# Layer 0's MLP: down products by features with the weights stationary, and 1/mean of squares as a row at the end

## The chip, the cores and the metric

The kernel runs on one core of one Trainium2 chip. The engines of the core are TensorE (PE in the profile, with its weight loads as PEld), VectorE (DVE), ScalarE (ACT), GpSimd (POOL) and SyncE (SP, which here only starts transfers). The metric is the device time of one execution in microseconds; the kernel before took a median of 1022.83 us in three runs (1022.65 to 1023.12).

## What is computed

A two-layer encoder over 512 tokens of 1024 features, in fp32. Layer 0 mixes tokens by stick-breaking attention, layer 1 by a gated linear recurrence (RG-LRU); each layer ends with a squared-ReLU MLP of 4096 hidden features. What the change touches is the MLP of layer 0 and the first step of layer 1:

```python
def rms_norm(x, g):
    y = x * rsqrt(mean(x * x, axis=-1) + EPS)
    return y * g

def squared_relu_mlp(h, w1, w2):
    u = relu(h @ w1)
    return (u * u) @ w2

for layer in range(2):
    h = rms_norm(x, norm_mix[layer])
    x = x + (attention(h) if layer == 0 else rglru_block(h))   # rglru_block begins with h @ w_in
    h = rms_norm(x, norm_mlp[layer])
    x = x + squared_relu_mlp(h, mlp_w1[layer], mlp_w2[layer])
return rms_norm(x, norm_final)
```

The factor of the norm is one number per token. Since ReLU and the square are applied to each element, `(u * u) @ w2` may be computed from x without the factor, and the product multiplied by 1/mean of squares, token by token, at its end. That is how both kernels do it.

## The kernel before

**Precision and layout.** Every matrix product is made of fp32 numbers split in two halves of a shorter type (`wh`, `wl` of the weights; a high and a low half of the activations), and takes three matmuls: high × high, low × high, high × low. Activations are held by features: `x[c]` is a tile of 128 features by 512 tokens, eight tiles in all, and tokens fall into a lower and an upper half of 256.

**The MLP.** It runs in four quarters of the hidden features. Each quarter does its up products (x to hidden) and its down products (hidden to output) by a scheme with seven products of half-size blocks, P1 to P7, in place of eight. The seven down products of a quarter are made in two pieces each (`g` is 0 or 1), in the order P1 0, P5 0, P1 1, P2 0, P5 1, P6 0, P6 1, P3 0, P3 1, P7 0, P7 1, P2 1, P4 0, P4 1: 14 pieces a quarter, 56 in layer 0. Each product ends in a PSUM bank pair named X, V or W, and is collected into one of four accumulators: P1 and P2 into `c[0]`, P6 and P3 into `c[1]`, P4 into `c[2]`, P5 and P7 into `c[3]`. P1, P6, P7 and P4 build on the same bank pair X one after the other, so the next of them can start only when the one before is collected.

**Down pieces before.** `part` (L1175, matmul at L1190) has the activations stationary and 512 columns of weights moving: 12 matmuls a piece, with a result of tokens by features. `collect` (L1154) adds the PSUM bank, times the factor of each token (a column of `rr`, one number per partition), to `c[out]` on VectorE; the first collect of an accumulator is a scaled copy on ScalarE (L1163). Layer 1's MLP uses the same functions (`mixed`) and keeps them in the change.

**The end of the MLP before.** The last product P4 of the last quarter is made in two halves of tokens by `times` (L1140, matmul at L1149). `feature(c)` (L1518) then brings one feature tile back: four TensorE transposes (L1522) of 128 by 128 into a PSUM bank, `add_x` (L764) adds them to x[c] on VectorE, and `halves` (L132) makes the high half `xgh` on ScalarE (L135) and the low half `xgl` on VectorE (L136) for the next product. Tiles 4 to 7 are done between the two halves of P4; tiles 0 to 3 inside the next stage, as entries of the table that `beside` (L246) takes. Squares for the next norm are summed by `squares.chunk` (L153), partly on GpSimd (L162).

**What follows.** `beside` makes the first two slabs of layer 1's input projection (`w_in`, matmuls at L234 to L236, slab casts at L227 and L229), feature tiles in the order 4 to 7, 0 to 3; then a third slab into another bank, with the norm's sum over features (L1655) inside it.

**What sets the order.** TensorE's order is as written. On VectorE and ScalarE of the MLP, `Ordered` (L784) puts each instruction behind the one before it, so they run in the order of the code as well; all its operations show the one line L793. Weights arrive by transfers on SyncE's queue; the sums of weight blocks that P7 and P4 need arrive partly by accumulating transfers that GpSimd issues (L1131). x waits in DRAM (`away`, written by `between` at L1540) during the MLP and is loaded again at L1547 in the last quarter. An operand made of weights lies at a column offset of 0, `UP_AT` = 16 or `OPEN_AT` = 36 in a slightly larger tile.

## Time and profile before

| | |
|---|---|
| timed, median of 3 runs | 1022.83 us |
| the profiled execution | 1023.47 us |
| span of its trace | 1021.7 us |
| granted TensorE clock | 0.998 of full |
| HBM traffic | 140.56 MB read, 6.29 MB written |

The span is what the trace covers from the first to the last instruction; the profiled execution's own time lies 1.8 us above it. The profile lists the busy time of each engine, a chain of work (followed back from the last instruction, at each step to what released it), groups of instructions by line, and a timeline of each engine. In a timeline row stand the start, the duration, the engine, the line, the operation and its tiles; a bracket gives the idle time ahead of the row and what ended it. Where a row says x2, the duration covers two instructions. Durations include a part in which the engine can already start its next instruction, so rows follow each other a little closer than they last.

### The profile page before, as it was taken

The page shows a single profiled execution, that of the slowest core. Times are in us where ns is not written, and L with a number is a line of the kernel's source. Part 1 is how long each engine was busy: PE and PEld are TensorE (multiplying, and loading weights), DVE is VectorE, ACT ScalarE, POOL GpSimd, SP SyncE. Part 2 cuts the span into 40 slices and gives each one's busy share as a digit, 9 for nine tenths or more (in the row PEclk, how much of TensorE's full clock was granted, in tenths as well). Part 3 has the DMA queues.
Part 4 walks back from the last instruction along what each step waited for, and adds up shares of the span by engine and source line. Part 5 has one row for each costly group of instructions (what it writes and reads, how often), then busy time and mean ns, then how long its engine had stood idle before and what let it go on. Part 6 is the DMA issues. An engine that isn't in the chain of part 4 may idle for free.

```text
span 1021.7 us, 16053 instructions
## 1 busy us (share of the span) xinstructions
PE 1013.0 (99%) x5930; PEld 890.1 (87%) x5930; DVE 868.3 (85%) x1165; ACT 701.5 (69%) x1081; POOL 175.5 (17%) x239
## 2 busy tenths in 40 slices
PE   9999999999999999999999999999999999999997
PEld 8888888888888988988988888888988988988986
DVE  7988787848789799799799888899898898898897
ACT  7777676835767764764775799966873763873866
POOL 0454344420000011011011221100010010010012
PEclk9999999999999999999999999999999999999999
DMA  7745454537536666676783476446767667667653
GB/s 237 222 122 145 115 152 102 152 111 262 160 81 198 166 156 195 166 158 194 166 230 90 118 192 173 116 170 200 214 112 206 165 143 202 173 142 201 168 106 111
DMA packets 58719, 165.73 MB, mean 162 GB/s; under 512 B 6928, under 2 KB 12304, under 8 KB 58640
## 3 DMA queue, kind: packets, MB, share of 16 engines
q1 hardware_dynamic: 47264, 124.41, 37.5%
q0 software_dynamic: 10944, 39.85, 23.4%
q8 instruction: 47, 0.77, 0.3%
q10 hardware_dynamic: 432, 0.44, 0.1%
q14 instruction: 32, 0.26, 0.1%
HBM read 140.56 MB, written 6.29 MB: 144 GB/s over the span
## 4 chain that ended last, share of the span: by engine, by line
PE 93%; ACT 3%; DVE 2%; DMA 1%; issue 1%; POOL 0%; ACTq 0%; DVEq 0%
PE ps_t L1190 16%; PE ps_acc L1055 9%; PE ps_acc L1190 9%; PE ps_z L1055 8%; PE ps_acc L234 5%; PE ps_acc L236 5%; PE ps_acc L235 5%; PE ps_o L1055 5%; PE ps_z L1190 4%; PE ps_t L234 2%; PE ps_t L236 2%; PE ps_t L235 2%; PE ps_o L234 2%; PE ps_o L236 2%; PE ps_o L235 2%; PE ps_t L628 2%
## 5 line engine op out<-in xcount | busy, mean ns | idle before, releaser
L793 ACT CAST wh<-b 128x1024 fp32r<-128x1024 f32 x174 | 180.3, 1051 | 121.6 <-DVE b L793 76.7
L793 DVE TENSOR_TENSOR wl<-b,wh 128x1024 fp32r<-128x1024 f32 x174 | 210.4, 1220 | 38.7 <-ACT wh L793 37.5
L1131 POOL DMA_DIRECT2D b<-in_w_dn x40 | 35.0, 875 | 295.3 <-DVE b L793 198.6
L234 PE MATMUL ps_acc<-xgh,wh 128*128 128x512 f32 x192 | 78.4, 408 | 0.0
L793 ACT ACTIVATE u<-u 128x512 f32<-128x512 f32 x103 | 64.9, 632 | 15.3 <-DVE u L793 13.5
L236 PE MATMUL ps_acc<-xgl,wh 128*128 128x512 f32 x192 | 75.2, 392 | 0.0
L235 PE MATMUL ps_acc<-xgh,wl 128*128 128x512 f32 x192 | 75.1, 391 | 0.0
L1131 POOL DMA_DIRECT2D b<-in_w_up x26 | 22.7, 872 | 291.7 <-DVE b L793 100.7
L606 DVE TENSOR_TENSOR_SCAN scan<-keep,later 128x128 f32<-128x128 f32 (+1 forms) x64 | 58.7, 918 | 15.4 <-POOL w L600 7.6
L793 DVE TENSOR_TENSOR b<-b,b 128x1024 f32<-128x1024 f32 x50 | 61.2, 1224 | 1.3
L610 POOL TENSOR_TENSOR w<-w,scan 128x128 f32<-128x128 f32 (+1 forms) x64 | 53.0, 830 | 53.4 <-DVE scan L606 48.8
L793 DVE TENSOR_TENSOR u<-u 128x512 f32<-128x512 f32 (+1 forms) x89 | 55.0, 618 | 4.4 <-ACT u L793 2.5
L229 DVE TENSOR_TENSOR wl<-raw,wh 128x512 fp32r<-128x512 f32 (+2 forms) x64 | 54.3, 877 | 4.1 <-ACT wh L227 4.0
L793 ACT CAST wh<-raw 128x1024 fp32r<-128x1024 f32 x49 | 51.2, 1048 | 6.8 <-PE ps_acc L1190 2.9
L227 ACT CAST wh<-raw 128x512 fp32r<-128x512 f32 (+2 forms) x64 | 44.4, 732 | 14.8 <-PE ps_acc L236 7.3
L1055 PE MATMUL ps_z<-xgh,wh 128*128 128x256 f32 x216 | 50.6, 277 | 0.2
L793 DVE TENSOR_TENSOR wl<-raw,wh 128x1024 fp32r<-128x1024 f32 x39 | 48.0, 1230 | 0.8 <-ACT wh L793 0.8
L1190 PE MATMUL ps_t<-wh,bh 128*128 128x512 f32 x120 | 47.0, 392 | 0.0
L1190 PE MATMUL ps_t<-wh,bl 128*128 128x512 f32 x120 | 46.8, 390 | 0.0
L600 POOL TENSOR_SCALAR_AFFINE_SELECT w<-w 128x128 f32<-128x128 f32 x64 | 32.9, 513 | 69.9 <-ACT w L595 69.7
L1055 PE MATMUL ps_acc<-low,wh 128*128 128x256 f32 x192 | 44.7, 276 | 0.0
L793 DVE TENSOR_TENSOR sl<-u,sh 128x512 fp32r<-128x512 f32 (+2 forms) x53 | 37.9, 716 | 7.7 <-ACT sh L793 7.7
(419 smaller groups left out, 3215.9 us busy)
## 6 DMA issues: line engine op xcount, KB each, us to landing
b<-in_w_dn SPq DMA_DIRECT2D x48, 512.0 KB, 4.3
b<-in_w_dn POOLq DMA_DIRECT2D x40, 512.0 KB, 5.6
b<-in_w_up SPq DMA_DIRECT2D x39, 512.0 KB, 4.6
b<-in_w_up POOLq DMA_DIRECT2D x26, 512.0 KB, 5.5
raw<-in_w_dn SPq DMA_DIRECT2D x16, 512.0 KB, 4.6
raw<-in_w_in SPq DMA_DIRECT2D x16, 512.0 KB, 3.7
raw<-in_w_up SPq DMA_DIRECT2D x13, 512.0 KB, 4.0
raw<-in_w_qk SPq DMA_DIRECT2D x12, 512.0 KB, 3.8
```

The costliest lines, as they stand in the source:

```text
L227: e[0].copy(wh[:, k, :], raw[:, k, :])
L229: e[1].tensor_tensor(wl[:, k, :], raw[:, k, :], f(wh[:, k, :]), ALU.subtract)
L234: PE.matmul(ps, wh, ah, start=start, stop=False)
L235: PE.matmul(ps, wl, ah, start=False, stop=False)
L236: PE.matmul(ps, wh, al, start=False, stop=stop)
L600: G.affine_select(t, t, pattern=[[-1, P]], compare_op=ALU.is_gt, fill=0.0, base=0, channel_multiplier=1,)
L606: V.tensor_tensor_scan(sc[:, S - n : S][:, ::-1], keep[:, :n][:, ::-1], later[:, S - n :][:, ::-1], 1.0, ALU.mult, ALU.max,)
L610: G.tensor_tensor(wt, wt, sc[:, S - n + 1 : S + 1], ALU.mult)
L793: ins = getattr(self.e, name)(*args, **kwargs)
L1055: PE.matmul(ps[:, i * HS : (i + 1) * HS], m, y, start=new and i == k == low == 0 and y is h, stop=(low, i, k) == steps[-1], skip_group_che ...
L1131: G.dma_start(out=unit[b].rearrange("p j n -> p (j n)"), in_=unit["src"](to), accum_op=ALU.add)
L1190: PE.matmul(sums[to][i], a[:, j, block, i * P : (i + 1) * P], y[:, j, :], start=new and g == j == n == 0 and a is h, stop=g == j == 1 and ...
```

## The change

In layer 0 alone (`not self.mixed`), the down products are turned round. `across` takes 128 by 128 blocks of weights as the stationary operand and 256 tokens of activations as the moving one: 24 matmuls of 256 columns a piece instead of 12 of 512. The result is by features, as x is, so no transposes remain (`feature` goes). The factor of a token then no longer belongs to a partition but to a column: `keep_factors` stores the factors in DRAM, `back` loads them as a row repeated on all 128 partitions (`rr`), and the accumulators, now summed without factors by plain additions and subtractions, are multiplied by that row once, in the last quarter, and added to x in blocks. `done(name)` does this after P6 (c[2], on GpSimd, with its four additions to x), after P3 (c[1], likewise), after P7 (c[3], product on VectorE) and after P2 (c[0], product on GpSimd; the additions of c[3] on VectorE). P4's own result is multiplied in PSUM and added by VectorE in `end`. GpSimd's MLP work, transfers included, becomes `Ordered` too.

```diff
--- before.py
+++ after.py
@@ -832,7 +832,8 @@
         def __init__(self, ctx, layer, squares=None):
             self.layer, self.sq, self.first = layer, squares or Squares(), None
             self.mixed = squares is not None
-            self.V, self.A = Ordered(V), Ordered(A)
+            self.V, self.A, self.G = Ordered(V), Ordered(A), Ordered(G)
+            self.G.turn(not self.mixed)
             self.mp = ctx.enter_context(tc.tile_pool(name=f"mlp{layer}", bufs=2))
             self.u = {}
             if self.mixed:
...
@@ -1136,6 +1137,23 @@
 
         FAR = "P7", "P4"
 
+
+        def across(self, name, g, i, w, ps, new=False, ends=True, rounds=None):
+
+            block = self.PRODUCTS[name][0]
+            (wh, wl), (h, l) = w, self.a[g]
+            rounds = rounds or [((h, wh), (l, wh)), ((h, wl),)]
+            for n, pairs in enumerate(rounds):
+                for jj in range(2):
+                    for a, y in pairs:
+                        for k in range(2):
+                            f0 = (2 * i + k) * P
+                            PE.matmul(
+                                ps[:, k * HS : (k + 1) * HS], y[:, jj, f0 : f0 + P], a[:, jj, block, :],
+                                start=new and n == jj == k == 0 and a is h,
+                                stop=ends and (n, jj, k) == (len(rounds) - 1, 1, 1),
+                                skip_group_check=name not in ("P1", "P5", "P2"),
+                            )
 
         def times(self, name, g, i, w, ps, new, cols=slice(0, S)):
 
@@ -1154,6 +1172,14 @@
         def collect(self, name, i, ps, cols=slice(0, S)):
             out, less = self.PRODUCTS[name][4:]
             y = self.c[out][:, i, cols]
+            if not self.mixed:
+                if (out, i) in self.begun:
+                    op = ALU.subtract if less else ALU.add
+                    self.gained = self.V.tensor_tensor(y, y, ps, op)
+                else:
+                    self.begun.add((out, i))
+                    A.activation(y, ps, AF.Identity, scale=1.0 - 2.0 * less)
+                return
             t = NB * less + out // 2 * 2 + i
             scale = self.rr[:, t : t + 1]
             if (out, i) in self.begun:
@@ -1183,6 +1209,14 @@
             rounds = ((h, wh), (l, wh)), ((h, wl),)
             if (name, g) == ("P1", 1):
                 rounds = ((h, wh),), ((h, wl),), ((l, wh),)
+            if not self.mixed:
+                for n in range(len(rounds)):
+                    for i in range(2):
+                        self.across(
+                            name, g, i, w, sums[to][i], new and g == n == 0,
+                            g == 1 and n == len(rounds) - 1, rounds[n : n + 1],
+                        )
+                return
             for n, pairs in enumerate(rounds):
                 for i in range(2):
                     for j in range(2):
@@ -1246,7 +1280,7 @@
                     return
                 name = steps[i][3]
                 kind, q4, p, name = steps[i]
-                at = 0
+                at = 0 if self.mixed else self.OPEN_AT if i == 0 else UP_AT
                 if kind == "up":
                     at = self.OPEN_AT if i == 0 or (p, name) == (0, "P1") else UP_AT
                 ws[i] = made[i] = self.operand(self.source(unit(i), name), at)
@@ -1324,6 +1358,8 @@
                     if p:
                         for n in range(2):
                             self.collect(name, n, bank[n])
+                        if not self.mixed and q4 == NQ - 1:
+                            end.done(name)
                     if not ahead:
                         prepare_or_hold(i)
                     if begin:
@@ -1457,9 +1493,13 @@
                 if new:
                     banks[to] = self.bank()
                 self.up(name, ws.pop(i), banks[to], new)
+            rest = [ws[len(steps) - 2 + g] for g in range(2)], sums["down", NQ - 1, 0]["X"]
+            if not self.mixed:
+                end(*rest)
             for e in (self.V, self.A):
                 e.turn(False)
-            end([ws[len(steps) - 2 + g] for g in range(2)], sums["down", NQ - 1, 0]["X"])
+            if self.mixed:
+                end(*rest)
 
         def mixed_quarters(self, residues, gains, end):
             self.gains = gains
@@ -1497,6 +1537,7 @@
                         self.sq.chunk(n, x[n], e=V)
                 if c == C - 2:
                     self.rr = self.sq.inv_squares(self.bank())
+                    between.factors(self.rr)
                 between(c)
 
                 k = c - 4
@@ -1515,48 +1556,106 @@
         squares = Squares()
         last = {}
 
-        def feature(c, tag):
-
...
+        factors = dram.tile([1, S], F32, tag="factors", name="factors")
+        lo, hi = slice(0, HS), slice(HS, S)
+        rr = []
+
+        def keep_factors(cols):
+            nc.sync.dma_start(
+                out=factors.rearrange("o (t p) -> p (o t)", p=P), in_=cols[:, :NB]
+            )
+
+        def back():
+            for c in (*range(4), *range(4, C)):
+                x[c] = home_tile(*HOMES[c], "x")
+                nc.sync.dma_start(out=x[c], in_=away[:, c, :])
+                if c == 0:
+                    rr.append(mlp.mp.tile([P, S], F32, tag="low", name="rr", bufs=1))
+                    nc.sync.dma_start(out=rr[0], in_=factors.broadcast_to([P, S]))
+
+        def times_factors(e, y, ts):
+            n = y.shape[1] // HS
+            y = y.rearrange("p (k n) -> p k n", k=n)
+            e.tensor_tensor(y, y, rr[0][:, ts].unsqueeze(1).broadcast_to([P, n, HS]), ALU.mult)
+
+        def add_block(e, out, ks=range(4)):
+            h, ts = out % 2, (lo, hi)[out // 2]
+            for k in ks:
+                xc = x[4 * h + k][:, ts]
+                e.tensor_tensor(xc, xc, mlp.c[out][:, k // 2, k % 2 * HS : (k % 2 + 1) * HS], ALU.add)
+
+        def block(out):
+            times_factors(mlp.G, mlp.c[out].rearrange("p i n -> p (i n)"), (lo, hi)[out // 2])
+            add_block(mlp.G, out)
+
+        def done(name):
+            if name == "P6":
+                block(2)
+            elif name == "P3":
+                block(1)
+            elif name == "P7":
+                times_factors(mlp.V, mlp.c[3].rearrange("p i n -> p (i n)"), hi)
+            elif name == "P2":
+                times_factors(mlp.G, mlp.c[0].rearrange("p i n -> p (i n)"), lo)
+                add_block(mlp.V, 3)
+
+        def high(*cs):
+            for c in cs:
+                mlp.A.activation(
+                    xgh[:, c, :], x[c], AF.Identity, scale=col("mix1")[:, c : c + 1]
                 )
-            add_x(c, pt)
-            last["low"] = halves("mix1", c, x[c])
+
+        def low(*cs):
+            for c in cs:
+                last["low"] = mlp.V.scalar_tensor_tensor(
+                    xgl[:, c, :], x[c], col("mix1")[:, c : c + 1], f(xgh[:, c, :]),
+                    ALU.mult, ALU.subtract,
+                )
+
+        def square(*cs):
+            for c in cs:
+                squares.chunk(c, x[c], e=G, a=mlp.A)
 
         def end(ws, xs):
             for i in range(2):
                 for g in range(2):
-                    mlp.times("P4", g, i, ws[g], xs[i], False)
-                mlp.collect("P4", i, xs[i])
...
+                    mlp.across("P4", g, i, ws[g], xs[i], ends=g == 1)
+
+            def add_last(i):
+                for k in range(2):
+                    xc = x[2 * i + k][:, hi]
+                    mlp.V.tensor_tensor(xc, xc, xs[i][:, k * HS : (k + 1) * HS], ALU.add)
+
+            high(4, 5, 6, 7)
+            low(4, 5)
+            add_block(mlp.V, 0, range(2))
+            low(6, 7)
+            square(4, 5)
+            times_factors(mlp.V, xs[0], hi)
+            add_last(0)
+            high(0)
+            square(6)
+            high(1)
+            times_factors(mlp.V, xs[1], hi)
+            add_block(mlp.V, 0, range(2, 4))
+            add_last(1)
+            low(0, 1)
+            square(7)
+            high(2, 3)
+            low(2, 3)
 
         def between(c):
             nc.sync.dma_start(out=away[:, c, :], in_=x[c])
             if c == C - 1:
                 soft.send(mlp.ready)
 
-        def back():
-            for c in range(C):
-                x[c] = home_tile(*HOMES[c], "x")
-                nc.sync.dma_start(out=x[c], in_=away[:, c, :])
-
-        end.ready = back
+        between.factors = keep_factors
+        end.ready, end.done = back, done
         mlp.quarters(between, end)
 
         begin = [bank("acc") for _ in range(2)]
         beside(
-            [slab(w_in[C + i]) for i in range(2)], xgh, xgl, begin,
-            {
-                1: lambda: [feature(c, "z") for c in range(2)],
-                2: lambda: [feature(c, "o") for c in range(2, 4)],
-            },
-            (*range(4, C), *range(4)),
+            [slab(w_in[C + i]) for i in range(2)], xgh, xgl, begin, {}, (*range(4, C), *range(4)),
         )
         behind[0] = last["low"].ins
         third = slab(w_in[C + 2])
```

Three places show how the instructions now stand. First VectorE at the end of the last quarter, from the collects of P7 on; `x_6399` to `x_6405` are x[4] to x[7], `ps_t` is bank pair X, `ps_z` W. Before:

```order
L793 SCALAR_TENSOR_TENSOR c3_3173<-ps_t_5913,rr_3514,c3_3173 128x512
L793 SCALAR_TENSOR_TENSOR c3_3173<-ps_t_5914,rr_3514,c3_3173 128x512
L229 TENSOR_TENSOR wl_6202<-raw_6199,wh_6201 128x1024
L793 SCALAR_TENSOR_TENSOR c0_3170<-ps_z_5973,rr_3514,c0_3170 128x512
L793 SCALAR_TENSOR_TENSOR c0_3170<-ps_z_5974,rr_3514,c0_3170 128x512
L229 TENSOR_TENSOR wl_6208<-raw_6205,wh_6207 128x1024
L793 SCALAR_TENSOR_TENSOR c2_3172<-ps_t_5913,rr_3514,c2_3172 128x512
L765 TENSOR_TENSOR x_5891<-x_5891,ps_z_6140 128x512
L765 TENSOR_TENSOR x_5893<-x_5893,ps_z_6150 128x512
L765 TENSOR_TENSOR x_5895<-x_5895,ps_o_6161 128x512
L765 TENSOR_TENSOR x_5897<-x_5897,ps_o_6172 128x512
L136 SCALAR_TENSOR_TENSOR xgl_83<-x_5891,colt_70,xgh_82 128x512
```

and now:

```order
L793 TENSOR_TENSOR c3_3173<-c3_3173,ps_t_6421 128x512
L793 TENSOR_TENSOR c3_3173<-c3_3173,ps_t_6422 128x512
L229 TENSOR_TENSOR wl_6886<-raw_6883,wh_6885 128x1024
L793 TENSOR_TENSOR c3_3173<-c3_3173,rr_6391 128x1024
L793 TENSOR_TENSOR c0_3170<-c0_3170,ps_z_6517 128x512
L793 TENSOR_TENSOR c0_3170<-c0_3170,ps_z_6518 128x512
L229 TENSOR_TENSOR wl_6892<-raw_6889,wh_6891 128x1024
L793 TENSOR_TENSOR x_6399<-x_6399,c3_3173 128x256
L793 TENSOR_TENSOR x_6401<-x_6401,c3_3173 128x256
L793 TENSOR_TENSOR x_6403<-x_6403,c3_3173 128x256
L793 TENSOR_TENSOR x_6405<-x_6405,c3_3173 128x256
L793 SCALAR_TENSOR_TENSOR xgl_83<-x_6399,colt_70,xgh_82 128x512
```

The collects lose their factor; the multiplication of c[3] comes in behind the first `wl`, and the additions to x[4] to x[7] are of SBUF operands, 256 wide, and stand ahead of P4's result instead of behind transposes.

Second GpSimd, from the last weight transfers to layer 1. Before:

```order
L1131 DMA b11_5530<-in_w_dn 128x1024
L1131 DMA b11_5534<-in_w_dn 128x1024
L162 TENSOR_TENSOR ssq_6148<-ssq_6148,sq_6158 128x512
L162 TENSOR_TENSOR ssq_6148<-ssq_6148,sq_6169 128x512
L162 TENSOR_TENSOR ssq_6148<-ssq_6148,sq_6180 128x512
L1585 MEMSET gh_6324 128x768
L1585 MEMSET gl_6325 128x768
```

and now:

```order
L793 DMA b11_6040<-in_w_dn 128x1024
L793 TENSOR_TENSOR c2_3172<-c2_3172,rr_6391 128x1024
L793 TENSOR_TENSOR x_6389<-x_6389,c2_3172 128x256
L793 TENSOR_TENSOR x_6393<-x_6393,c2_3172 128x256
L793 TENSOR_TENSOR x_6395<-x_6395,c2_3172 128x256
L793 TENSOR_TENSOR x_6397<-x_6397,c2_3172 128x256
L793 TENSOR_TENSOR c1_3171<-c1_3171,rr_6391 128x1024
L793 TENSOR_TENSOR x_6399<-x_6399,c1_3171 128x256
L793 TENSOR_TENSOR x_6401<-x_6401,c1_3171 128x256
L793 TENSOR_TENSOR x_6403<-x_6403,c1_3171 128x256
L793 TENSOR_TENSOR x_6405<-x_6405,c1_3171 128x256
L793 TENSOR_TENSOR c0_3170<-c0_3170,rr_6391 128x1024
```

Behind the same last transfer three products of 1024 and eight additions of 256 are put in; the sums of squares follow as before.

Third ScalarE, from the casts of the `w_in` slabs to the high halves of x[4] to x[7]. Before:

```order
L227 CAST wh_6201<-raw_6199 128x1024
L227 CAST wh_6207<-raw_6205 128x1024
L135 ACTIVATE xgh_82<-x_5891,colt_70 128x512
L157 ACTIVATE ssq_6148<-x_5891 128x512
L135 ACTIVATE xgh_82<-x_5893,colt_70 128x512
L160 ACTIVATE sq_6158<-x_5893 128x512
L135 ACTIVATE xgh_82<-x_5895,colt_70 128x512
L160 ACTIVATE sq_6169<-x_5895 128x512
L227 CAST wh_6293<-raw_6291 128x1024
L135 ACTIVATE xgh_82<-x_5897,colt_70 128x512
```

and now:

```order
L227 CAST wh_6885<-raw_6883 128x1024
L227 CAST wh_6891<-raw_6889 128x1024
L227 CAST wh_6945<-raw_6943 128x1024
L793 ACTIVATE xgh_82<-x_6399,colt_70 128x512
L793 ACTIVATE xgh_82<-x_6401,colt_70 128x512
L793 ACTIVATE xgh_82<-x_6403,colt_70 128x512
L793 CAST wh_7017<-raw_6982 128x1024
L793 ACTIVATE xgh_82<-x_6405,colt_70 128x512
L793 ACTIVATE ssq_6853<-x_6399 128x512
L793 ACTIVATE sq_6855<-x_6401 128x512
```

The third cast has moved ahead of the high half of x[4], and the squares behind the high halves.

17 lines of the change are left out of this document (4 added, 13 removed).

## The prediction

> **What bounds the kernel now.** First the page: which engine is busy, and which engine the last chain of work runs over.
>
> ```profile
> span 1021.7 us, 16053 instructions
> PE 1013.0 (99%) x5930; PEld 890.1 (87%) x5930; DVE 868.3 (85%) x1165; ACT 701.5 (69%) x1081; POOL 175.5 (17%) x239
> PE 93%; ACT 3%; DVE 2%; DMA 1%; issue 1%; POOL 0%; ACTq 0%; DVEq 0%
> ```
>
> TensorE (PE) is busy 99% of the span and carries 93% of the chain. So there are two ways to change the time: take matmul time away, or make PE wait where it doesn't wait now. The second is open because VectorE (DVE) is busy 85% on average and may be full where the change lies. I therefore read the chain in order of time around the end of layer 0's MLP (start, duration, work).
>
> ```profile
> 539.01 5.57 PE ps_acc L1190 x24
> 544.58 5.44 PE ps_t L1190 x24
> ...
> 552.74 2.72 PE ps_t L1149 x12
> 555.46 0.87 PE ps_z L1522 x8
> 556.34 0.87 PE ps_o L1522 x8
> 557.21 2.75 PE ps_t L1149 x12
> 559.96 0.23 PE ps_acc L234
> ...
> 561.32 0.87 PE ps_z L1522 x8
> ...
> 563.58 0.87 PE ps_o L1522 x8
> ...
> 572.66 0.23 PE ps_t L234
> ```
>
> The reader is to see that PE has no gap: the last down products (L1190), P4 in two halves (L1149), four groups of transposes (L1522), then at 559.96 the first matmul of layer 1's input projection (L234), and at 572.66 the first of its third slab. One row of 5.57 instead of 5.44 is a small wait.
>
> Then VectorE over the same stretch, from its timeline.
>
> ```profile
> 537.97 1.41 DVE L793 SCALAR_TENSOR_TENSOR c<-ps_acc,rr,c 128x512 f32<-128x512 f32 x2
> 539.28 0.68 DVE L793 TENSOR_TENSOR sl<-u,sh 128x512 fp32r<-128x512 f32 x1
> 539.88 1.22 DVE L793 TENSOR_TENSOR wl<-b,wh 128x1024 fp32r<-128x1024 f32 x1
> 541.02 0.68 DVE L793 TENSOR_TENSOR sl<-u,sh 128x512 fp32r<-128x512 f32 x1
> 541.62 1.22 DVE L793 TENSOR_TENSOR wl<-b,wh 128x1024 fp32r<-128x1024 f32 x1
> 542.76 1.41 DVE L793 SCALAR_TENSOR_TENSOR c<-ps_t,rr,c 128x512 f32<-128x512 f32 x2
> 544.08 1.22 DVE L793 TENSOR_TENSOR wl<-b,wh 128x1024 fp32r<-128x1024 f32 x1
> 545.21 1.22 DVE L793 TENSOR_TENSOR wl<-raw,wh 128x1024 fp32r<-128x1024 f32 x1
> 546.35 1.41 DVE L793 SCALAR_TENSOR_TENSOR c<-ps_acc,rr,c 128x512 f32<-128x512 f32 x2
> 547.66 2.35 DVE L793 TENSOR_TENSOR wl<-b,wh 128x1024 fp32r<-128x1024 f32 x2
> 549.93 1.41 DVE L793 SCALAR_TENSOR_TENSOR c<-ps_t,rr,c 128x512 f32<-128x512 f32 x2
> 551.25 1.22 DVE L229 TENSOR_TENSOR wl<-raw,wh 128x1024 fp32r<-128x1024 f32 x1
> 552.38 1.41 DVE L793 SCALAR_TENSOR_TENSOR c<-ps_z,rr,c 128x512 f32<-128x512 f32 x2
> 553.71 1.22 DVE L229 TENSOR_TENSOR wl<-raw,wh 128x1024 fp32r<-128x1024 f32 x1
> ```
>
> No row shows idle time in brackets: VectorE is full for 16 us, one instruction behind the other, and it is the engine to which the change adds work just there. From start to start a 512 row takes 0.60, a 1024 row 1.14, a pair of collects 1.31. GpSimd (POOL), which gets the rest of the new work, is idle there:
>
> ```profile
> 559.35 3.48 POOL L162 TENSOR_TENSOR ssq<-ssq,sq 128x512 f32<-128x512 f32 x2 [21.15 <-ACT sq L160]
> ```
>
> **The matmuls.** Each of the 56 down pieces of layer 0 becomes 24 matmuls of 256 columns, where it was 12 of 512. The old piece costs 5.44 / 2 = 2.72 (the x24 row holds two pieces). The up pieces are 24 matmuls of 256 already, with weights stationary, as the new ones will be:
>
> ```profile
> 432.60 2.72 PE ps_o L1055 x24
> 726.84 2.87 PE ps_z L1055 x24
> ```
>
> So 2.72 for 2.72: I take nothing for this part. The other end is 0.15 for each of 56 pieces, +8.4 us, if all ran like the second row. That is one of the few up pieces whose weights lie 36 columns into their tile; the new pieces use the other offset except the very first, so I stay at the first row.
>
> The Trainium skill (TensorE: Matmul & The Clock Gate, "Wait — 56ns, not 53.3ns?") puts a fixed 2.5 ns on each matmul of a warm array. By that rule 12 more matmuls a piece would cost 30 ns, 1.7 us in all; the rows with 2.72 on both sides don't show it.
>
> **What goes.** The four groups of transposes go: 4 × 0.87 = 3.48 us on the path, 1.74 ahead of 559.96 and 1.74 behind it. The collects become plain additions of one PSUM operand and one SBUF operand; at the 0.60 of a 512 row a pair takes 1.20, where it took 1.31. That shortens the small waits of the kind of 5.57 (three of about 0.1 in the trace), some 0.3 in all, hidden elsewhere by PE's full rows.
>
> **What comes.** The factor row goes through DRAM on the sync queue: one small store early in the MLP and one broadcast load beside the reloads of x (about 512). It has 25 us until its first use, about 538; nothing for it. If it came later than that, GpSimd alone would wait.
>
> On GpSimd: c2 × factors (1024 elements a partition), four additions of 256 into x, c1 × factors, four additions, c0 × factors. On VectorE: c3 × factors and twelve 256-wide additions, two multiplications in PSUM. The trace prices GpSimd's two-operand work at up to 512 elements:
>
> ```profile
> L610 POOL TENSOR_TENSOR w<-w,scan 128x512 f32<-128x512 f32 x16 | 18.3, 1142 | 15.3 <-DVE scan L606 14.8
> L610 POOL TENSOR_TENSOR w<-w,scan 128x384 f32<-128x384 f32 x16 | 15.9, 992 | 18.7 <-DVE scan L606 17.6 <-DMA raw<-in_w_qk 1.0
> L738 POOL TENSOR_TENSOR x<-x,early 128x512 f32<-128x512 f32 x2 | 2.6, 1292 | 9.4 <-DMA x<-in_xT 9.4
> ```
>
> With about 0.19 fixed, this is 1.86 ns an element by the first row ((1142 − 190) / 512; some 1.76 in its undisturbed instances) and 2.15 by the third: a 1024 product 2.0 to 2.4 us, a 256 addition 0.64 to 0.74. From 384 to 512 the w rows grow by only 1.17 ns an element, the low end. The third row has the new work's form (in place, added to x), and I take 2.15.
>
> Alone this would be hidden. It isn't alone: GpSimd and VectorE hold each other up. When GpSimd worked on 512 elements at 92.06, the VectorE instruction that began at 92.41 took 1.58, where its like take 0.68:
>
> ```profile
> 92.06 1.39 POOL L610 TENSOR_TENSOR w<-w,scan 128x512 f32<-128x512 f32 x1 [1.69 <-DVE scan L606]
> L229 DVE TENSOR_TENSOR wl<-raw,wh x4: 668/683/1584, 91.8 to 95.7; 128x512 fp32r<-128x512 f32 x4
> ```
>
> (Columns of the second: minimum, median, maximum in ns.) That is 0.90 longer, nearly all that GpSimd had left (1.04). It goes both ways, but not for VectorE instructions with an operand in PSUM:
>
> ```profile
> 1001.96 1.99 POOL L793 TENSOR_TENSOR c<-c,gb 128x512 f32<-128x512 f32 x1 [5.12 <-ACT junk L1858]
> 1008.50 1.50 POOL L793 TENSOR_TENSOR c<-c,gb 128x512 f32<-128x512 f32 x1 [4.54 <-ACT junk L1858]
> ...
> 1002.72 1.41 DVE L793 SCALAR_TENSOR_TENSOR c<-ps_t,rr,c 128x512 f32<-128x512 f32 x2
> ```
>
> Here the pair from PSUM took its usual 1.41 beside GpSimd (whose 1.99 waited for a wl row first; alone it takes 1.50, which is 2.56 ns an element, the high end). So I read: of two-operand instructions with both operands in SBUF one engine runs at a time; GpSimd holds VectorE off for its duration less about 0.2 (2.2 for a product, 0.55 for an addition). In the stretch above, wl and sl rows are of that kind, collects aren't.
>
> The Trainium skill (GPSIMD Engine Reference, section 8, "Key points") says that the two share their SBUF interfaces and contend on VectorE instructions with two SBUF inputs: the rows just quoted agree. Its section 3.1 gives 2.6 cycles an element at 1.2 GHz for such work, 2.17 ns: the x row agrees, the w rows are below it and the c row above. By 2.17 the sum below would stay as it is.
>
> **The sum.** When does x[4], the first operand of the input projection, have its last addition (c3's)? In the new order VectorE does, from the sl at 539.17 (0.1 earlier by a cheaper collect): 2 sl × 0.60 + 8 wl × 1.14 + 8 collects × 0.60 + c3 × factors 1.14 + one 256 addition 0.4 (half of 0.60, and the 0.1 by which a row outlasts its start-to-start). 1.20 + 9.12 + 4.80 + 1.14 + 0.4 = 16.7, so 555.9 undisturbed. Holds by GpSimd on top: c2's product begins near 537.8, beside the collects of 537.97, and holds the sl for 1.0; three of c2's additions 3 × 0.55 = 1.65 (the fourth falls beside the collects from PSUM); c1's product 2.2; of its additions 0.6, the rest beside collects; c0's product 2.2, right ahead of the addition that x[4] waits for. Together 7.65: 563.5. (By the w rows' 1.76, products hold 1.8 and additions 0.45: 0.6 + 1.35 + 1.8 + 0.5 + 1.8 = 6.05, 1.6 less.) Then the high half of x[4] on ScalarE:
>
> ```profile
> 556.88 0.72 ACT L135 ACTIVATE xgh<-x,colt 128x512 fp32r<-128x512 f32 x1 [3.96 <-DVE x L765]
> 558.56 1.41 DVE L136 SCALAR_TENSOR_TENSOR xgl<-x,colt,xgh 128x512 fp32r<-128x512 f32 x2
> ```
>
> 0.63 of the 0.72 go by until the next can start: the input projection begins at about 564.1, where it began at 559.96: **+4.1**. PE meanwhile, which would be ready 1.74 earlier, waits: some 1.9 ahead of P7 (the bank of X is free only when c1's late collect is done), 1.0 ahead of P4, 3.6 ahead of the projection.
>
> Behind it, PE ran 572.66 − 559.96 = 12.70 to the third slab, 1.74 of it transposes: 10.96 stay. The low half of x[4] comes 0.5 after the first high matmuls want it (0.75 for a row like the xgl one). x[0]'s is the next risk: from xgl of x[4] to xgl of x[0] VectorE has about 7.9 us of rows (the halves, c0's additions, PSUM products and P4's additions, one hold by a square's sum), PE 6.4 us of matmuls: 1.6 of wait. 564.1 + 10.96 + 0.5 + 1.6 = 577.2, against 572.66: **+4.5**; a tenth more for the norm behind the later squares: **+4.6**. From there PE was full before and is full after: the 4.6 stay to the end. The profiled execution took 1023.47 in all (span 1021.7 and 1.8 around it), 0.64 above the median of the runs shown, 1022.83. 1023.47 + 4.6 = 1028.1 for a profiled run, **1027.4** for the median.
>
> **The rivals.**
>
> *GpSimd gets in nobody's way* (the holds are much shorter for these shapes, or VectorE goes first). Then x[4] is ready near 556.6 and the projection waits only for the cast of the third w_in slab, which ScalarE does ahead of the high halves and which waits for P4's first weights: about 558.2, so −1.74 is kept, about 1.1 of wait for x[0] eats the larger part of the second 1.74, and the 0.3 comes on top: −2.3, **1020.5**, faster. For it: the transposes are real matmul time, and PE bounds. Against it: the three holds quoted. 0.12.
>
> *Shorter holds*, from the low end of 1.17 ns an element up to 1.7: at the low end products hold 1.2 and additions 0.3, c2's product none, together 0.9 + 1.2 + 0.3 + 1.2 = 3.6, 4 less than above: +0.6; up to +2.5 at 1.7. **1024**. 0.13.
>
> *Longer holds*, the high end of 2.56 ns (the c row is a product too): products hold 2.6, additions 0.65, together 1.4 + 1.95 + 2.6 + 0.8 + 2.6 = 9.35, 1.7 more than above; and as VectorE falls behind, up to four more additions meet wl rows instead of collects, 2.6 more. +6.3 to +8.9, **1031**. 0.09.
>
> *Dearer narrow matmuls*: +8.4 by the 2.87 row on top of a sum at either price of GpSimd, **1034**. 0.03.
>
> *The change doesn't do what it says*: if the orders kept the transposes' place filled with another wait, it is the sum above; nothing in the order leaves the transposes in. No chance of its own.
>
> **How the numbers follow.** The forecast (holds of 1.76 to 2.4 ns) has 0.63, 1025.8 to 1029.5. What a measurement of this kernel can tell is about 0.2%, 2.05 us: faster is below 1020.8, slower above 1024.9. Of the no-contention case most is faster, 0.12 with a little of its upper half at same; of the short-hold case two thirds lie within: same 0.10; the rest, 0.78, is slower. The range takes the forecast, the short holds and the better part of the long ones, and leaves out the no-contention case and the narrow matmuls: 1023.0 to 1031.0.
>
> **What would show it.** No transposes, and down pieces of 24 still at 2.72; GpSimd products of 2.0 to 2.4 (3.3 where they wait for VectorE); wl rows of 1.7 to 3.4 instead of 1.22 between 538 and 558; PE waits ahead of P7, of P4, and of 3 to 4 us ahead of the projection's first matmul, released by ScalarE's high half; that matmul at 564 and the third slab at 577. The prediction is wrong if wl rows stay at 1.22 beside busy GpSimd, if the projection starts before 560, or if down pieces leave 2.72.

## The result, and the profile after

The changed kernel took a median of 1028.93 us (1028.61 to 1029.88, 4 runs), the kernel before 1022.98 us (1022.65 to 1023.28, 4 runs): a ratio of 1.0061 with a 95% interval of 1.0046 to 1.0075, 5.95 us slower. The profiled execution took 1029.19 us, 5.72 more than that of before. Every time in this document leaves out one slow execution, the first one of the kernel `vector_psum` further down, which took 5827.59 us with TensorE at about a sixth of its speed.

The page of the kernel after, the lines that answer to the first ones of before:

```profile
PE 1012.8 (99%) x6570; PEld 915.3 (89%) x6570; DVE 874.2 (85%) x1170; ACT 700.8 (68%) x1081; POOL 194.7 (19%) x250
PE 91%; DVE 4%; ACT 2%; DMA 1%; issue 1%; POOL 0%; SPq 0%; DVEq 0%; ACTq 0%
```

The busy time says almost nothing: PE 1012.8 against 1013.0, although 3.48 us of transposes are gone. GpSimd was busy 19 us longer, its own waits for VectorE included. The chain tells more: VectorE's share went from 2% to 4%, and ScalarE's and PE's shrank. Where PE waited, from the view of its waits (line, what it waited for, us in total, times, longest), two rows of the MLP's end are new:

```profile
PE ps_acc L234 <- ACT xgh L793: 3.3, 1, 3.3
PE ps_t L1151 <- DVE c L793: 2.2, 2, 1.8
```

The chain in order of time shows where VectorE stands on it:

```profile
539.67 3.08 PE ps_acc L1151 x24
542.78 0.97 DVE wl L793
...
546.58 0.61 DVE c L793
547.32 2.72 PE ps_t L1151 x22
...
562.10 3.48 DVE x L793 x4
565.59 0.67 DVE xgl L793
...
581.39 0.86 PE ps_z L1754 x2
```

and the norm's matmuls in the same view of the kernel before:

```profile
575.38 0.86 PE ps_z L1655 x2
```

They begin at 581.39 instead of 575.38: 6.01 late, as much as the whole loss. Then VectorE and GpSimd over that stretch, from their timelines:

```profile
538.84 1.28 DVE L793 TENSOR_TENSOR c<-c,ps_acc 128x512 f32<-128x512 f32 x2
540.03 2.03 DVE L793 TENSOR_TENSOR sl<-u,sh 128x512 fp32r<-128x512 f32 x1
541.99 1.76 DVE L793 TENSOR_TENSOR wl<-b,wh 128x1024 fp32r<-128x1024 f32 x1
543.67 1.22 DVE L793 TENSOR_TENSOR sl<-u,sh 128x512 fp32r<-128x512 f32 x1
544.82 1.76 DVE L793 TENSOR_TENSOR wl<-b,wh 128x1024 fp32r<-128x1024 f32 x1
...
551.16 4.57 DVE L793 TENSOR_TENSOR wl<-b,wh 128x1024 fp32r<-128x1024 f32 x2
...
558.02 1.75 DVE L793 TENSOR_TENSOR c<-c,rr 128x1024 f32<-128x1024 f32 x1
...
562.02 3.56 DVE L793 TENSOR_TENSOR x<-x,c 128x256 f32<-128x256 f32 x4
```

```profile
538.76 2.75 POOL L793 TENSOR_TENSOR c<-c,rr 128x1024 f32<-128x1024 f32 x1
541.59 5.57 POOL L793 TENSOR_TENSOR x<-x,c 128x256 f32<-128x256 f32 x4
551.32 3.33 POOL L793 TENSOR_TENSOR c<-c,rr 128x1024 f32<-128x1024 f32 x1 [4.16 <-DVE c L793]
554.72 5.64 POOL L793 TENSOR_TENSOR x<-x,c 128x256 f32<-128x256 f32 x4
561.04 3.25 POOL L793 TENSOR_TENSOR c<-c,rr 128x1024 f32<-128x1024 f32 x1 [0.68 <-DVE c L793]
```

Read the two against each other: while GpSimd's first product runs (538.76 to 541.51), VectorE's collects from PSUM keep their 1.28 a pair, and the first instruction with two SBUF operands behind them takes 2.03 instead of 0.68. During the four additions the wl rows take 1.76 instead of 1.22 and the sl row 1.22 instead of 0.68; during the second product two wl rows take 4.57 instead of 2.35; during the third four additions of 256 take 3.56. And GpSimd is slowed by VectorE as well: an addition takes 1.4 on average, about twice the 0.64 to 0.74 that it was priced at alone.

Last, what was not forecast: windows (us, busy time of PE, PEld, DVE, ACT, POOL, then the granted clock, DMA share, GB/s) around the start of the input projection at 565.44:

```profile
562.16:565.43 3.27, 0.01 (x1) 0.00 (x0) 3.27 (x4) 0.77 (x2) 2.14 (x1) 1.00 0.50 160
565.43:570.60 5.17, 5.03 (x14) 3.70 (x15) 5.14 (x11) 4.33 (x7) 1.27 (x1) 0.67 0.01 3
```

and the same columns for two stretches of 3.41 us:

```profile
563.64:567.05 3.41, 1.48 (x5) 0.97 (x6) 3.41 (x7) 2.39 (x4) 0.66 (x1) 1.00 0.34 130
567.05:570.46 3.41, 3.41 (x9) 2.64 (x9) 3.38 (x8) 2.57 (x5) 1.17 (x1) 0.50 0.00 0
```

PE idles for 3.27 us, and over the next 5.17 its clock is 0.67 on average: it goes on at 1.00 until 567.05 and then runs at 0.50 for 3.41 us, so that 1.7 us of matmul time are lost.

### The profile page after: what moved, and what is told of

It reads as the page before. It is cut to its first block, busy times and chain, and to the rows that moved or that the text cites. A ratio compares the mean times of both kernels' runs of the same rounds, so it can differ in the third digit from the quotient of the medians.

```text
span 1027.4 us, 17362 instructions
## 1 busy us (share of the span) xinstructions
PE 1012.8 (99%) x6570; PEld 915.3 (89%) x6570; DVE 874.2 (85%) x1170; ACT 700.8 (68%) x1081; POOL 194.7 (19%) x250
## 4 chain that ended last, share of the span: by engine, by line
PE 91%; DVE 4%; ACT 2%; DMA 1%; issue 1%; POOL 0%; SPq 0%; DVEq 0%; ACTq 0%
PE ps_acc L1056 9%; PE ps_z L1056 8%; PE ps_t L1224 8%; PE ps_t L1151 8%; PE ps_acc L236 5%; PE ps_acc L234 5%; PE ps_acc L235 5%; PE ps_o L1056 5%; PE ps_acc L1224 4%; PE ps_acc L1151 4%; PE ps_t L234 2%; PE ps_t L236 2%; PE ps_t L235 2%; PE ps_z L1224 2%; PE ps_z L1151 2%; PE ps_o L234 2%
## 5 line engine op out<-in xcount | busy, mean ns | idle before, releaser
L793 DVE TENSOR_TENSOR wl<-b,wh 128x1024 fp32r<-128x1024 f32 x174 | 213.9, 1240 | 40.5 <-ACT wh L793 40.3
L234 PEld LDWEIGHTS ps_acc<-xgh,wh 128*128 128x128 f32 x192 | 36.6, 190 | 8.7 <-ACT xgh L793 3.5
L236 PEld LDWEIGHTS ps_acc<-xgl,wh 128*128 128x128 f32 x192 | 36.3, 189 | 8.7 <-DVE xgl L793 0.7
```

The lines of the kernel that those rows point to most:

```text
L234: PE.matmul(ps, wh, ah, start=start, stop=False)
L236: PE.matmul(ps, wh, al, start=False, stop=stop)
L793: ins = getattr(self.e, name)(*args, **kwargs)
```

## The experiments

### GpSimd's blocks left out of the change

```diff
-            if name == "P6":
-                block(2)
-            elif name == "P3":
-                block(1)
+            if name in ("P6", "P3"):
+                pass
...
-                times_factors(mlp.G, mlp.c[0].rearrange("p i n -> p (i n)"), lo)
```

> The changed kernel without the GpSimd blocks: the products of c[0], c[1], c[2] with the factor row and the additions of c[1] and c[2] to x are left out (so x is not the reference's). Theory A (GpSimd holds VectorE off whenever both have two operands in SBUF): the wl rows between 540 and 556 go back to 1.14 to 1.22, x[4] is complete some 7.9 us earlier (the sum of the holds in the trace after), the projection waits only for the third w_in cast and begins near 559 to 560, its clock stays at 1.00; 1021.5 to 1023. Rival B (VectorE's own new rows and the new order on ScalarE make the projection late, GpSimd is beside the point): the projection still begins after 563; 1027 or more. Rival C (the narrow matmuls cost it): 1027 or more, with PE waits gone.

Measured: 1022.50 us (1021.24 to 1025.32, 10 runs), a ratio to before of 0.9998 [0.9988, 1.0007]. The rows of VectorE between 539 and 556 are back at their usual durations (timeline of this run):

```profile
539.35 0.68 DVE L793 TENSOR_TENSOR sl<-u,sh 128x512 fp32r<-128x512 f32 x1
539.95 1.22 DVE L793 TENSOR_TENSOR wl<-b,wh 128x1024 fp32r<-128x1024 f32 x1
...
547.49 2.35 DVE L793 TENSOR_TENSOR wl<-b,wh 128x1024 fp32r<-128x1024 f32 x2
...
552.12 1.22 DVE L793 TENSOR_TENSOR c<-c,rr 128x1024 f32<-128x1024 f32 x1
...
555.59 1.42 DVE L793 TENSOR_TENSOR x<-x,c 128x256 f32<-128x256 f32 x4
```

The waits ahead of P7, P4 and the projection are gone; the one left is of 1.4 us, for the low half of x[0]. So GpSimd's blocks carry the loss, 6.4 us, as A says; B and C fall. But the kernel isn't faster than before either, though work is missing: in this order of things the change can't win even without those blocks.

### GpSimd's blocks added to the kernel before

```diff
+        def same(y):
+            n = y.shape[1] // P
+            y = y.rearrange("p (k n) -> p k n", k=n)
+            mlp.G.tensor_tensor(y, y, ones.unsqueeze(1).broadcast_to([P, n, P]), ALU.mult)
+
+        def done(name):
+            out = {"P6": 2, "P3": 1, "P2": 0}.get(name)
...
+            same(mlp.c[out].rearrange("p i n -> p (i n)"))
+            if out:
+                for k in range(4):
+                    same(x[4 * (out % 2) + k][:, out // 2 * HS : (out // 2 + 1) * HS])
```

> The kernel before, with GpSimd work of the new size and place added and nothing else: after P6 a product of c[2] (1024 wide) and four of 256 on x[0] to x[3], after P3 the same on c[1] and x[4] to x[7], after P2 a product of c[0], all by ones. Theory A: VectorE's wl and sl rows there stretch by the same 7 to 8 us in all, TensorE waits ahead of P7, P4 and the transposes; 3 to 5 us slower, 1026 to 1028. Rival B: within 0.3 us of the kernel before.

Measured: 1027.67 us (1027.36 to 1028.23, 4 runs) beside 1022.92, a ratio of 1.0048 [1.0033, 1.0063]: 4.75 us, with none of the rest of the change. The timelines of VectorE and GpSimd:

```profile
538.37 4.65 DVE L793 TENSOR_TENSOR sl<-u,sh 128x512 fp32r<-128x512 f32 x1
```

```profile
536.97 2.76 POOL L793 TENSOR_TENSOR c<-c,ones 128x1024 f32<-128x1024 f32 x1
539.38 3.08 POOL L793 TENSOR_TENSOR x<-x,ones 128x256 f32<-128x256 f32 x4
```

One sl row of 0.68 stands still from 538.37 until GpSimd's product and its four additions are through, at 542.46. The additions take 0.77 each here, undisturbed, where in the change VectorE came in between each two of them. (The same five instructions behind P3, later in this run, did take turns with VectorE.) PE waits 1.94 for this sl row, then runs at 0.65 on average for 4.9 us (1.7 lost), and waits 0.85 once more: 4.5 together. The places differ from the change, the cause is the same.

### The same work on VectorE

```diff
-            times_factors(mlp.G, mlp.c[out].rearrange("p i n -> p (i n)"), (lo, hi)[out // 2])
-            add_block(mlp.G, out)
+            times_factors(mlp.V, mlp.c[out].rearrange("p i n -> p (i n)"), (lo, hi)[out // 2])
+            add_block(mlp.V, out)
...
-                times_factors(mlp.G, mlp.c[0].rearrange("p i n -> p (i n)"), lo)
+                times_factors(mlp.V, mlp.c[0].rearrange("p i n -> p (i n)"), lo)
```

> The changed kernel with the same products and additions on VectorE in place of GpSimd. Theory A: they cost VectorE 2 x (1.14 + 4 x 0.33) + 1.14 = 6.1 us of its own instead of 7.9 of being held, so the projection begins about 1.8 us earlier, near 563.6; 1026.5 to 1027.5, faster than the changed kernel although VectorE does all the work. Rival B (GpSimd's work was free, VectorE is the bound): 6 us later, 1034 or more.

Measured: 1027.93 us (1027.57 to 1029.27, 4 runs), 1.0 below the change by medians. That difference isn't clear of noise: the ratios to before are 1.0049 [1.0032, 1.0066] here and 1.0061 [1.0046, 1.0075] for the change. B, which asked for 1034, falls; A's 1026.5 to 1027.5 is missed by a little. The x[4] additions begin at 562.66, so x[4] is done some 1.5 us earlier than in the change, as expected. Most of it is given back on ScalarE, whose timeline says why:

```profile
562.01 1.06 ACT L227 CAST wh<-raw 128x1024 fp32r<-128x1024 f32 x1 [7.99 <-PE ps_t L1151]
563.42 1.05 ACT L793 CAST wh<-raw 128x1024 fp32r<-128x1024 f32 x1 [0.36 <-DVE x L793]
564.37 2.56 ACT L793 ACTIVATE xgh<-x,colt 128x512 fp32r<-128x512 f32 x4
```

Two casts stand ahead of the high half. The third w_in cast waited for P4's first weights to be used, and P4 was late: PE waited 2.56 for c[3]'s collect behind c[1]'s block, and ran at 0.58 on average for the 4.1 us behind it.

### The wait filled with matmuls

```diff
+            spare = bank("o")
+            for n in range(28):
+                PE.matmul(
+                    spare[:, :HS], ws[1][0][:, 0, :P], mlp.a[1][0][:, 0, 0, :],
+                    start=n == 0, stop=n == 27,
+                )
```

> The changed kernel with 28 extra matmuls of 256 columns (3.2 us) into a spare bank behind P4, where TensorE waits 3.3 us for x[4]. In the trace after, the granted clock of the 5.2 us behind that wait is 0.67. Theory D (the low clock follows the idle time, and took the place of the forecast wait for x[0]): the clock stays at 1.00, the projection's start stays near 565.4, a wait of 0.5 to 1 us for x[0] or its neighbours comes back; 0.5 to 1.0 us faster, 1028.0 to 1028.4. Rival E (all of the clock's 2 us is lost): 1026.5 to 1027. Rival F (the clock falls for another reason): 0.67 again and 1028.9.

Measured: 1028.97 us (1027.79 to 1031.02, 4 runs), beside 1028.93 for the change. The clock stays at 1.00 throughout, and the wait for x[0]'s low half is back:

```profile
574.99 0.50 PE L236 MATMUL ps_acc<-xgl,wh 128*128 128x512 f32 x1 [1.27 <-DVE xgl L793]
```

F falls (the clock fell for the idle time), E falls (the 1.7 us aren't to be had). D's mechanism holds. Its gain of 0.5 to 1.0 isn't seen, though times that scatter over 3 us couldn't show it either; the reason against it lies in the two traces. The low half of x[0] comes 7.9 us after the projection's start at either clock, from VectorE, and PE either waits for it or arrives late by itself. (In this trace the projection starts at 567.11, later than in the change: the layer began 1.2 us later, and more of its second quarter ran at the slow pace described below.)

### Down weights at column 0

```diff
-                at = 0 if self.mixed else self.OPEN_AT if i == 0 else UP_AT
+                at = 0
```

> The changed kernel with the down weights at column 0 of their tile, as the kernel before had them, instead of 16 (36 for the first). In the trace after, down pieces take 2.72, but 2.83 in most of the second quarter (0.5 us in all), and 2.87 the first. Theory N1 (the column offset sets the pace of narrow matmuls): the 2.83 rows go or become the rule, at 0.11 to 0.15 a piece: 1028.3, or up to 1035. Theory N2 (the slower pace begins behind a wait, whatever the column): the share of 2.83 rows changes by chance, within 0.7 us of 1028.9.

Measured: 1034.30 us (1033.32 to 1036.68, 4 runs), a ratio to before of 1.0111 [1.0098, 1.0125]: 5.4 us slower than the change by the medians, 5.1 by the two ratios. From the chain of this run, pieces of the first and the last quarter:

```profile
294.05 2.88 PE ps_acc L1151 x24
...
530.19 2.88 PE ps_acc L1151 x24
```

The pieces run at 2.88 instead of 2.72 in all four quarters; N1, with the slower pace as the rule. 56 pieces would make 9 us. Less came because the change already ran seven pieces of its second quarter at 2.83, and because behind P3 of the last quarter PE waits for VectorE anyway: the waits ahead of P7 and P4 shrank from 2.2 to 1.2 us. So the one line of the diff that moves the down weights to another column is worth some 5 us.

### Without GpSimd, put where VectorE has room

`vector_reordered` does all of it on VectorE, c[2]'s block already after P1, and x[4] first; `vector_reordered_w` also takes one low half of the weights from VectorE. The core of their edits:

```diff
+            if name == "P1":
+                times_factors(mlp.V, mlp.c[2].rearrange("p i n -> p (i n)"), hi)
+                add_block(mlp.V, 2)
+            elif name == "P7":
+                times_factors(mlp.V, mlp.c[1].rearrange("p i n -> p (i n)"), lo)
+                times_factors(mlp.V, mlp.c[3].rearrange("p i n -> p (i n)"), hi)
+                for k in range(2):
+                    add_block(mlp.V, 1, [k])
+                    add_block(mlp.V, 3, [k])
...
+                A.activation(wl, wh, AF.Copy, scale=-1.0)
+                G.dma_start(out=wl, in_=raw, accum_op=ALU.add)
```

> All scaling on VectorE, as in blocks_on_vector, but placed by where VectorE is needed: c[2]'s product and additions already behind P1 of the last quarter; c[1]'s and c[3]'s products behind P7's collect, then the additions tile by tile, x[4] first; c[0]'s product in two halves behind the low half of x[6]; the third w_in cast behind the high halves. Theory A (the holds are gone, and with them VectorE's chain to x[4] is about 16.7 - 0.4 + 2 products 2.3 + 2 additions 0.7, less the last collects): x[4] complete near 557, the projection begins when P4 ends, near 558.5 to 559.5, waits of about 1.3 us in all for the low halves of x[0] to x[3] remain; 1021 to 1023. Rival (any scaling at the end costs more than the transposes): 1024 or more.

> vector_reordered, and the low half of the first w_in slab no longer by VectorE: ScalarE writes the negative high half and an accumulating transfer of GpSimd's queue adds the raw weights. Theory A: 1.14 us less on VectorE ahead of the projection, the late low halves wait less; 0.5 to 1.2 us faster than vector_reordered, 1020.3 to 1022. Rival: the transfer (5.5 us from issue to landing) is late for the first weights, 1 to 2 us slower than vector_reordered.

Measured: 1029.57 us (1027.89 to 1030.14) and 1028.69 us (1027.27 to 1030.49), 5 runs each: both miss their forecasts by more than 6 us, and the ranges overlap too much to tell the two apart. PE's longest wait in the first (what it waited for, us in total, times, longest):

```profile
PE ps_t L1152 <- ACT wh L794: 2.3, 1, 2.3
```

VectorE had no room after P1. The block of 2.5 us there delayed the weights of the second P6 piece, PE waited 2.31 and then ran at 0.62 on average for 4.5 us. The bound on VectorE isn't at the layer's end alone.

`vector_psum` drops the early block, adds c[2] to P4's result in PSUM and takes both low halves from VectorE:

```diff
+            mlp.V.tensor_tensor(xs[0], xs[0], mlp.c[2][:, 0], ALU.add)
             times_factors(mlp.V, xs[0], hi)
```

> vector_reordered_w without the early block of c[2], which cost a wait of 2.3 us ahead of P6 there: c[2] is added to P4's result in PSUM instead (two additions of 0.60 more, one product of 1.14 and four additions of 0.33 less), and both w_in slabs get their low halves from ScalarE and transfers. Theory A: no wait ahead of P6, P7 or P4; x[4] is complete near 556, the projection begins when P4 ends, near 558.5; VectorE's rows from there to the low half of x[3] are still about 1 to 2 us longer than TensorE's 11 us, so waits of 1 to 2 us for x[0] to x[3]: 1021.5 to 1023.5, about the kernel before. Rival (the transfers' landing decides, 5.5 us behind ScalarE's rows at 553 to 554): the projection waits at its second slab until 560.5 or later; 1024 to 1025.

Measured: a median of 1024.41 us in 11 runs (1022.71 to 1025.32), a ratio to before of 1.0011 [1.0002, 1.0020]: 4.5 us faster than the change, and still not faster than before. For its rows the kernel was run once more:

> The same kernel as vector_psum, for a trace: the profiled execution there ran its whole length with TensorE at about a sixth of its speed (1.28 us for a matmul of 512 columns), so that its rows say nothing on the waits. Theory A: no wait ahead of P6, P7, P4, the projection near 558.5 to 559.5, waits of 1 to 3 us in all for the low halves of x[0] to x[3], about 1024. Rival: the wait is for the low half of a w_in slab.

```profile
559.95 0.50 PE L236 MATMUL ps_acc<-xgh,wl 128*128 128x512 f32 x1 [0.48 <-DMA wl<-raw]
569.00 0.50 PE L235 MATMUL ps_acc<-xgh,wh 128*128 128x512 f32 x1 [1.50 <-ACT xgh L794]
```

1023.58 us, beside 1023.84 for the kernel before, one run each. PE runs through to the projection; two waits are left inside it, 1.98 together, about as long as the transposes that stood there before (1.74). The last run reordered these steps:

> vector_psum with the last steps in the order in which TensorE needs them: x[2] and x[3] are completed tile by tile ahead of the low halves that can wait, the squares of x[4] to x[7] and their sums stand behind all halves (no GpSimd sums among VectorE's rows), the norm two tiles later in the third slab, the first down piece at the same column offset as the others. Theory A: the wait of 1.5 us for the high half of x[2] in vector_psum_again goes, and 0.15 of the first piece; 0.5 of wait for the first w_in slab's low half stays: 1.0 to 1.6 us faster than vector_psum, 1022.4 to 1023.4, within 0.1% of the kernel before. Rival (the sums of squares are late for the norm, and the norm's wait replaces it): 1024 or more.

Measured: 1025.75 us (1025.20 to 1027.63, 8 runs), 1.3 slower than vector_psum. The wait for x[2] went, as expected; the rival came with it, and one thing that no theory had. The waits (a view of PE) and the chain at the layer's start:

```profile
PE ps_z L1763 <- DVE ssq L162: 1.2, 1, 1.2
PE ps_acc L236 <- DMA wl<-raw: 0.8, 1, 0.8
```

```profile
291.04 2.83 PE ps_t L1152 x24
293.87 2.83 PE ps_acc L1152 x24
```

With the first piece at column 16 like the rest, all the first quarter runs at 2.83 a piece; with it at column 36 that piece takes 2.87 and the rest 2.72. From the first piece to the end of this quarter that is 39.58 us, where vector_psum_again took 38.24: the 1.3 us by which this version is slower. No version was clearly faster than the kernel before.

## Why the prediction was right, step by step

The forecast was 1027.4 (1023.0 to 1031.0), slower; 1028.93 came. By its own steps:

- **The matmuls, nothing.** True for most pieces, not for all: the first took 2.87, as its column offset had said, and the last seven of the second quarter ran at 2.83. From the chain of the change:

```profile
289.67 2.87 PE ps_t L1151 x24
...
386.00 5.88 PE ps_acc L1151 x48
391.88 5.65 PE ps_t L1151 x48
```

  and the same two stretches of the second quarter in the kernel before:

```profile
385.93 5.72 PE ps_acc L1190 x24
391.65 5.44 PE ps_t L1190 x24
```

  Beside the kernel before, the first quarter is 0.15 longer and the second 0.51; the third is 0.14 shorter, as a wait of 0.13 is gone. The first piece of P3 in the last quarter starts at 539.67, 0.66 later than before, and 0.10 of that was there when the layer's MLP began. From there on five pieces ran at 2.83 as well (PE's timeline, the first rows of P7 1 and P2 1, 2.83 apart):

```profile
550.22 0.40 PE L1151 MATMUL ps_t<-sh,wh 128*128 128x256 f32 x2
...
553.05 0.40 PE L1151 MATMUL ps_z<-sh,wh 128*128 128x256 f32 x2
```

  They cost nothing, as PE waits for VectorE there; they only make its waits shorter than forecast. By the prediction's own list, down pieces that leave 2.72 were a sign of being wrong, and this sign came true in part. The rival of dearer narrow matmuls is real, but the offset in the change keeps most of it off; down_at_0 shows its price.
- **The holds, 7.65.** Measured, each row less its usual duration: 2.03 − 0.68 = 1.35 on the first sl (1.0 forecast); 3 × 0.54 = 1.62 for the additions (1.65); 4.57 − 2.35 = 2.22 for c[1]'s product (2.2); 1.75 − 1.22 = 0.53 (0.6); 3.56 − 1.42 = 2.14 for c[0]'s product (2.2). 7.86 in all. The price of 2.15 ns an element was the right row, and the rule (SBUF pairs exclude each other, PSUM doesn't) held for shapes that the trace of before didn't have. Removing the cause and adding it alone settle that it is the cause. One row was misread, without harm to the sum: the c×gb product of 1.50 that gave the high end of 2.56 ns wasn't alone, since a wl row of VectorE from 1007.62 ran 0.34 us into it; the next one, at 1010.48, takes 1.30, which is 2.17 ns an element.
- **PE's waits.** 1.9 ahead of P7, 1.0 ahead of P4, 3.6 ahead of the projection were forecast; 1.76, 0.43 and 3.27 came. The projection began at 565.44, not 564.1: VectorE's stretch began 0.86 later than forecast (540.03 for 539.17), the holds were 0.2 more, and the first matmul came 0.78 behind the start of the high half (564.66), not 0.63. In the 0.86 are the 0.66 above and some 0.2 from a weight transfer that landed later: ScalarE waited 2.33 for it ahead of its cast at 530.75, where before it waited 1.21.
- **Behind the projection's start, 0.5 and 1.6.** The size held, the mechanism was incomplete: of the wait for x[0] 0.17 came (at its weight load), since PE was slowed by the clock in its place, 1.7 us. That the idle time would lower the clock wasn't forecast. filled_wait, where the clock stays up and PE waits 1.27 for x[0], shows that the slow clock cost little or nothing here, as VectorE's low half of x[0] sets the time either way.
- **To the end.** 6.01 late at the norm, 5.7 at the end of the span (1027.4 for 1021.7): what was late there stayed, as forecast.

So the term that was mis-sized most is the first one: 0 for the narrow matmuls, where the first two quarters took 0.66 more. The norm came 1.4 later than forecast (6.01 for 4.6). PE's lateness at P3 makes 0.66 of it, the transfer some 0.2, the holds 0.2, the step from high half to matmul 0.15; the last 0.2 isn't taken apart.

Of the rivals, GpSimd in nobody's way asked for 1020.5; with GpSimd's blocks gone the kernel took 1022.5, so even that case was rated too well: its wait for x[0] is 1.4 (1.1 forecast), and by P3 its slow pieces had cost 0.5. That rival's own terms (−1.74, −0.64 and −0.3) also add up to −2.7, not to the −2.3 that it states.

## What to carry to other kernels

Before work is given to an idle engine, look at what its neighbour does in that stretch: here a product that VectorE does in 1.14 us held VectorE up for 2.2 from GpSimd. Taking matmul time from a full TensorE pays only as far as the engine that feeds it has room at that very place, and a busy share of 85% over the span says nothing of that; a timeline without brackets does. And when a stationary operand moves, compare its column offset as well as its shape: the same 24 matmuls took 2.72 us with their weights at column 16 and 2.88 at column 0.

## What the runs showed of the hardware

- GpSimd and VectorE don't share evenly. In before_with_gpsimd a product and four additions of GpSimd, each beginning before the one ahead of it had ended, kept VectorE out over five in a row (4.65 us for one row of 0.68). The same five instructions behind P3 of that run took turns with VectorE: the product took 4.46 beside two wl rows at their usual 2.34, where undisturbed it takes 2.42. What decides the turn wasn't tried.
- The granted clock is decided in slots of 3.41 us, and half a slot of idle time is enough for a fall. In each trace the falls begin a whole number of slots behind the clock's first rise (in the change at 567.05, 165 slots behind 3.85), and each is a clock of 0.50 for one slot, 1.7 us of matmul time; in down_at_0 it lasted two, 6.83 us. In the slots ahead of the seven falls (the one at the very end of each kernel not counted) TensorE had worked 0.85 to 1.70 us of the 3.41; no fall came behind a slot in which it had worked 1.91 or more. Why the clock stayed down for a second slot in down_at_0 isn't shown. The two closest to the line, from vector_reordered_w (a fall follows) and from filled_wait (none does):

```profile
570.42:573.83 3.41, 1.70 (x6) 0.96 (x6) 2.95 (x6) 1.44 (x3) 1.36 (x1) 1.00 0.20 32
```

```profile
545.07:548.48 3.41, 1.91 (x17) 1.71 (x16) 3.41 (x4) 1.05 (x1) 3.41 (x3) 1.00 0.00 0
```

  So the length of one wait doesn't decide. Of two waits of 1.94 one gave a fall (before_with_gpsimd) and the other didn't (filled_wait), and so with two of 1.66 (vector_reordered_w and vector_reordered): it matters how much of a wait lies in one slot. The Trainium skill (TensorE: Matmul & The Clock Gate, "What's actually happening") has the clock fall after an idle window of about 3.4 us, in windows that run freely. The length and the free running agree with these rows; but here a window half idle was enough, and all seven falls came after waits of less than 3.4 us, from 1.66 to 3.27.
- Matmuls of 256 columns have several paces. 24 of them took 2.72, 2.83 or 2.88 us at the same granted clock of 1.00. With the weights at column 0 the pace was 2.88 (down_at_0), at column 16 it was 2.72 or 2.83. The first quarter ran at 2.72 in the seven kernels whose first piece lies at column 36, and at 2.83 in the one where it lies at 16. In the second quarter the 2.83 began around 385 in four kernels and around 354 in filled_wait, behind short waits, and ended with the quarter's down products; in three others (blocks_on_vector, vector_reordered_w, vector_psum_again) it didn't set in for good. Why it begins and ends stays open.
